# Attention in another order: transposes and values two steps behind the scores and between their rows, scans in 256-column parts from a queue, six probability rows

## The chip, the cores and the metric

The kernel runs on one core of a Trainium2 chip. The number to explain is the device time of one execution in microseconds (us). The engines are named as in the profile: PE multiplies matrices (PEld is its weight load, which overlaps it), DVE is the vector engine, ACT the scalar engine, POOL is GpSimd, SP issues DMAs. Before the change three runs took 2288.64 to 2288.95 us, median 2288.77 us.

## What is computed

One decoder layer over 1024 tokens of width 1024 in float32: a half-weight SwiGLU block, two attentions side by side with gates, another half-weight SwiGLU block, and a gated embedding. The change touches the attentions. Both have 8 heads of width 64, and queries are taken in blocks of 128 rows.

```python
# forgetting attention (fox), causal
logits = q @ k.T * scale + F[t] - F[s]          # F: running sum of log forget gates
out = softmax(logits) @ v
# stick-breaking attention (sb), strictly causal
z = q @ k.T * scale
after = reverse_cumsum(log_sigmoid(-z)) - log_sigmoid(-z)
out = exp(log_sigmoid(z) + after) @ v
```

The kernel does the second in products instead of logarithms: `T = sigmoid(z)`, `G = sigmoid(-z)`, and a running product of G from the right by a scan on DVE. Each float32 operand of a matmul is split in a high and a low part.

## The kernel before, in words

The layer runs as one program: first SwiGLU block, gates, projections, attention, merge of the branches, second SwiGLU block, embedding. In the SwiGLU, gate and output stages the code fixes the order on every engine; in attention a planner orders each engine's queue from the order of the code, except where `order("pe", ...)`, `order("dve", ...)` and `order("act", ...)` chain instructions by hand. The chain on DVE holds the scans and, in stick-breaking heads, the low parts of the transposed probabilities.

Attention goes through 16 heads, h = 0 to 15: 8 fox heads and then 8 sb heads. A head has four steps, c = 0 to 3. A step has two parts:

- `scores` (L1015 on) for two rows of 128 queries, i = 2c and 2c + 1, each with n = 128(i + 1) keys. PE multiplies q by the high and the low part of k (L1037, L1038). A fox row is then added to the forget sums and reduced on DVE (L1042), goes through exp on ACT (L1048), a reciprocal on DVE (L1049) and a multiplication on POOL (L1050). An sb row has two sigmoids on ACT (L1045 writes G, L1046 writes T), a mask on POOL (L1052), the scans on DVE (L1013) from G into a third tile R, and multiplications T by R on POOL (L1060, L1064).
- `apply` (L1074 on) for a step whose rows T are finished. From the last 256 keys to the first, PE transposes a block of 2 x 256 probabilities into a PSUM bank (L1089), ACT copies its high part into the tile PT (L1091) and DVE writes the low part (L1092, "the low" below). There are c + 1 such turns in a step. The values matmuls (L1111) of a block stand two turns later. At the end ACT and DVE take the sum out of the one bank `av` (L1133, L1134).

Before the change the apply of a step stands behind both score rows of the next step. The scans of a row are cut into two parts, `right` and `left`; those of the first row of a step are issued at once, and those of the second row go into a list `later`, one part behind each turn's low. So the DVE order in a turn is: low, scan part, next low. Two PSUM banks hold transposes (`pt`), three hold scores (`sc`), and four tiles T hold probability rows, which is two steps.

Between these, `fill()` puts matmuls of other units (projections L799 and L807, branch products L1360) into the PE order, a share of the head's fill at each call. A step calls it 7, 4, 5 and 6 times for c = 0 to 3. What is left at the end of a head is run out.

## Time and profile before

| what | us |
|---|---|
| median of three runs | 2288.77 |
| the profiled execution, its own time | 2287.47 |
| its span | 2285.6 |
| fox heads, 851 to 1123, length | 272 |
| sb heads but the last, 1123 to 1357.8, length | 234.8 |
| last sb head and the apply behind it, 1357.8 to 1407 | 49.2 |

The profiled execution is 1.3 us below the median, and the span begins and ends inside it. The stages outside 851 to 1407 us have their order fixed by hand; the granted clock of PE is 1.00 of full speed throughout. In the profile's rows a matmul counts as busy until its modelled end, while the next one starts earlier: a row of several matmuls tells the distance between them.

### The profile page before, as it was taken

The numbers are of one execution on the slowest core, as the hardware profiler recorded it, in microseconds if no ns is written. First come the engines' busy times: TensorE is split into PE (matmuls) and PEld (weight loads), VectorE is DVE, ScalarE is ACT, GpSimd is POOL, SyncE is SP. The second block draws the span as 40 slices with busy tenths as digits, with TensorE's granted clock in tenths as the row PEclk, the third lists the DMA queues.
The fourth block names the chain that finished last, engine by engine and source line by source line (L and its number), as shares of the span: only waits on it lengthen the run. The fifth ranks groups of instructions, "written<-read, shape, count | busy, mean of one in ns | idle before, by whom it ended". The sixth has DMA issues, their size and how long they took to land.

```text
span 2285.6 us, 30594 instructions
## 1 busy us (share of the span) xinstructions
PE 2242.3 (98%) x11402; PEld 1900.6 (83%) x11402; DVE 1498.9 (66%) x2264; ACT 999.5 (44%) x1787; POOL 805.7 (35%) x747
## 2 busy tenths in 40 slices
PE   8999999999999999999999989999999999999999
PEld 6888888888888899998788778888888888888887
DVE  8845454688877336566578786888745555778753
ACT  6333333333365445565656663246333333434431
POOL 2444444300011236566457554500535343200121
PEclk9999999999999999999999999999999999999999
DMA  3232323474233342233223346732423232656132
GB/s 139 102 116 93 115 93 115 174 277 170 84 128 130 120 144 72 64 103 88 70 47 83 93 125 203 263 133 74 138 79 129 79 129 79 252 196 220 62 104 83
DMA packets 184902, 283.87 MB, mean 124 GB/s; under 512 B 27945, under 2 KB 104105, under 8 KB 184754
## 3 DMA queue, kind: packets, MB, share of 16 engines
q1 hardware_dynamic: 184752, 281.92, 37.1%
q8 instruction: 90, 1.47, 0.3%
q14 instruction: 58, 0.48, 0.1%
q10 hardware_dynamic: 2, 0.00, 0.0%
HBM read 189.83 MB, written 75.27 MB: 116 GB/s over the span
## 4 chain that ended last, share of the span: by engine, by line
PE 87%; DVE 7%; ACT 3%; issue 1%; POOL 1%; DMA 1%; SPq 0%; DVEq 0%; ACTq 0%; POOLq 0%
PE ps L556 39%; PE ps L454 21%; PE ps L799 7%; PE ps L1555 4%; PE ps L1360 3%; PE ps L807 3%; DVE RN L1013 3%; PE ps L1111 2%; PE ps L506 2%; PE ps L1089 2%; DVE PT L1092 1%; PE ps L1037 1%; PE ps L1038 1%; PE ps L956 1%; PE ps L228 1%
## 5 line engine op out<-in xcount | busy, mean ns | idle before, releaser
L454 PE MATMUL ps<-H,H 128*128 128x512 f32 x2184 | 497.7, 389 | 1.2 <-DVE X L462 1.2
L454 PEld LDWEIGHTS ps<-H,H 128*128 128x128 f32 x2184 | 409.3, 188 | 86.7 <-issue 2.0
L556 PE MATMUL ps<-H,WL 128*128 128x512 f32 x1116 | 265.0, 389 | 0.8 <-ACT WL L105 0.8
L556 PEld LDWEIGHTS ps<-H,WL 128*128 128x128 f32 x1116 | 209.4, 188 | 44.7 <-ACT WL L105 1.2
L556 PE MATMUL ps<-H,Q 128*128 128x512 f32 x612 | 146.0, 389 | 0.0
L462 DVE SCALAR_TENSOR_TENSOR X<-ps,X 128x512 f32<-128x512 f32 x168 | 109.0, 685 | 50.9 <-PE ps L454 50.9
L556 PEld LDWEIGHTS ps<-H,Q 128*128 128x128 f32 x612 | 114.9, 188 | 23.9
L556 PE MATMUL ps<-X,WL 128*128 128x512 f32 x552 | 132.6, 389 | 0.0
L1092 DVE TENSOR_TENSOR PT<-ps,PT 128x512 fp32r<-128x512 f32 (+1 forms) x160 | 99.9, 630 | 49.6 <-ACT PT L1091 48.8
L139 POOL TENSOR_TENSOR WL<-RAW,WH 128x512 fp32r<-128x512 f32 (+1 forms) x84 | 98.1, 1191 | 67.8 <-ACT WH L129 44.5
L556 PEld LDWEIGHTS ps<-X,WL 128*128 128x128 f32 x552 | 103.6, 188 | 21.5
L1111 PE MATMUL ps<-PT,X 128*128 128x256 f32 (+1 forms) x640 | 103.0, 286 | 15.3 <-DVE PT L1092 11.9
L799 PE MATMUL ps<-WH,H 128*128 128x256 f32 x768 | 115.6, 287 | 0.6 <-ACT PT L962 0.3
L807 PE MATMUL ps<-H,WH 128*128 128x512 f32 x384 | 114.9, 408 | 0.0
L1091 ACT CAST PT<-ps 128x512 fp32r<-128x512 f32 (+1 forms) x160 | 87.1, 549 | 61.6 <-PE ps L1089 60.2
L219 POOL TENSOR_SCALAR ss<-ss 128x1 f32<-128x1 f32 x28 | 8.4, 298 | 297.2 <-ACT WL L215 231.9
L1111 PEld LDWEIGHTS ps<-PT,X 128*128 128x128 f32 x640 | 89.8, 190 | 27.6 <-DVE PT L1092 18.2
L556 PE MATMUL ps<-H,PT 128*128 128x512 f32 x456 | 108.8, 389 | 0.0
L1013 DVE TENSOR_TENSOR_SCAN RN<-GF,RN 128x127 f32<-128x127 f32 (+2 forms) x96 | 102.6, 1068 | 2.5
L799 PEld LDWEIGHTS ps<-WH,H 128*128 128x128 f32 x768 | 101.4, 190 | 2.1 <-ACT PT L962 0.5
L1089 PE MATMUL ps<-identf,T 128*128 128x128 f32 x576 | 90.6, 275 | 11.6 <-DVE PT L1092 9.9
L1050 POOL TENSOR_TENSOR T<-T,l 128x128 f32<-128x128 f32 (+3 forms) x64 | 73.1, 1148 | 78.6 <-DVE l L1049 77.2
(434 smaller groups left out, 4825.4 us busy)
## 6 DMA issues: line engine op xcount, KB each, us to landing
hidden<-PT SPq DMA_DIRECT2D x40, 512.0 KB, 3.1
WH<-in_ffn_w_gate_dram SPq DMA_DIRECT2D x38, 512.0 KB, 5.3
Q<-hidden SPq DMA_DIRECT2D x24, 512.0 KB, 7.1
hidden<-RN SPq DMA_DIRECT2D x22, 512.0 KB, 2.6
KH<-in_ffn_w_up_dram SPq DMA_DIRECT2D x20, 512.0 KB, 6.2
KL<-in_ffn_w_up_dram SPq DMA_DIRECT2D x20, 512.0 KB, 6.9
T<-in_ffn_w_down_dram SPq DMA_DIRECT2D x20, 512.0 KB, 4.2
X<-in_x_dram SPq DMA_DIRECT2D x16, 512.0 KB, 9.5
```

What stands on the lines that cost most here:

```text
L139: ins = eng_lo.tensor_sub(lo[part], raw[part], f(hi[part]))
L454: pe(nc.tensor.matmul(groups[g][t][:], act[:, a, k, t * P:(t + 1) * P], wt[:, b, k, :], start=(fresh and n == 0), stop=(i in (6, 1, 4) and ...
L462: nc.vector.scalar_tensor_tensor(xs, groups[g][t][:], scale, xs, ALU.mult, ALU.add)
L556: pe(nc.tensor.matmul(ps[:], hl[:, a, k, :], rhs(m, b, k), start=(first and i == 0), stop=(final and i == 11), skip_group_check=True))
L799: pe(nc.tensor.matmul(ps[:, :n], hT[t // 4](a, k)[:, (t % 4) * P:(t % 4 + 1) * P], w[k // 4][b][:, k % 4, :n], start=(i == 0), stop=(i == ...
L807: pe(nc.tensor.matmul(ps[:], w[a][:, k, :], hT[half](b, k), start=(i == 0), stop=(i == 23)))
L1013: order("dve", nc.vector.tensor_tensor_scan(*args))
L1089: pe(nc.tensor.transpose(ps[:, col:col + P], step["pr"][j][:, kb * P:(kb + 1) * P], identf[:]))
L1091: high = nc.scalar.copy(pt[:, 0, :width], ps[:, :width])
L1092: low = nc.vector.tensor_sub(pt[:, 1, :width], ps[:, :width], f(pt[:, 0, :width]))
L1111: pe(nc.tensor.matmul(o, lh, r, start=(kpair == c and i == 0), stop=(kpair == 0 and i == 3)))
L1555: pe(nc.tensor.matmul(ps, hT[t // 4](a, k)[:, (t % 4) * P:(t % 4 + 1) * P], pl["w"][d, k // 2][b][:, k % 2, cs], start=(i == 0), stop=(i = ...
```

## The change

Seven things are changed, nearly all inside attention.

1. `apply` runs two steps behind `scores`, not one, and its turns stand between the two score rows: 1, 2, 1, 1 turns for c = 0 to 3, the rest behind the second row. `scores` and `apply` become generators for this.
2. The scans are cut at multiples of 256 keys. The parts wait in a list `pend`, sorted by step and then from the right. `pop` issues one part, or two when more than five wait: once before each score row and once in each turn, ahead of the low. Before a row all parts of the step two back are popped, and in a turn all parts that its transposes or the two turns behind it need.
3. A scan writes into G itself; the tile R goes. G takes turns between the two pools that held G and R, so four rows of G are there instead of two. The segments of an sb row are scored from the right.
4. There are six tiles T instead of four and four tiles PT instead of five; two tiles of the gate stage move from PT to T, and the scratch area for software DMA shrinks from 4096 to 1024 bytes.
5. The last addition of an apply (L1134 before) is issued later, behind the next low or ahead of the next score row; in sb heads it joins the DVE chain.
6. The fill of a head is shared out anew, 0.27, 0.19, 0.27, 0.27 over 6, 7, 4, 5 calls.
7. The last head gets five branch units as fill instead of seven; the other five run beside the two applies that remain at the end.

The number of instructions on PE, ACT and SP stays. DVE gets 32 more scans (192 instead of 160), POOL 56 more multiplications (160 instead of 104).

First place, DVE in step c = 3 of sb head h = 11. SCALAR_TENSOR_TENSOR on L1013 is a scan, TENSOR_TENSOR PT a low, KL the low part of a key stack, Y the last addition. Before:

```order
L1013 SCALAR_TENSOR_TENSOR RN_11496<-GF_11495,mask_sb 128x128
L1013 SCALAR_TENSOR_TENSOR RN_11496<-GF_11495,RN_11496 128x383
L882 TENSOR_TENSOR KL_11274<-ps_11427,KH_11273 128x512
L1013 SCALAR_TENSOR_TENSOR RN_11496<-GF_11495,RN_11496 128x384
L1092 TENSOR_TENSOR PT_11556<-ps_11552,PT_11556 128x384
L1013 SCALAR_TENSOR_TENSOR RN_11535<-GF_11534,mask_sb 128x128
L1013 SCALAR_TENSOR_TENSOR RN_11535<-GF_11534,RN_11535 128x383
L1092 TENSOR_TENSOR PT_11572<-ps_11567,PT_11572 128x512
L1013 SCALAR_TENSOR_TENSOR RN_11535<-GF_11534,RN_11535 128x512
L1092 TENSOR_TENSOR PT_11586<-ps_11581,PT_11586 128x512
L1134 TENSOR_TENSOR Y_10845<-ps_11551,Y_10845 64x256
```

And now, in the same step:

```order
L1013 SCALAR_TENSOR_TENSOR RN_11446<-RN_11446 128x256
L1013 SCALAR_TENSOR_TENSOR GF_11412<-GF_11412 128x255
L1117 TENSOR_TENSOR PT_11514<-ps_11510,PT_11514 128x384
L1013 SCALAR_TENSOR_TENSOR RN_11446<-RN_11446 128x255
L1013 SCALAR_TENSOR_TENSOR GF_11493<-GF_11493,mask_sb 128x128
L1013 SCALAR_TENSOR_TENSOR RN_11528<-RN_11528,mask_sb 128x128
L1013 SCALAR_TENSOR_TENSOR RN_11528<-RN_11528 128x128
L1117 TENSOR_TENSOR PT_11549<-ps_11544,PT_11549 128x512
L1013 SCALAR_TENSOR_TENSOR GF_11493<-GF_11493 128x256
L1013 SCALAR_TENSOR_TENSOR RN_11528<-RN_11528 128x256
L1163 TENSOR_TENSOR Y_10800<-ps_11509,Y_10800 64x256
```

Three turns with their lows stood in this step and stand in the next head's first step now; of the rows' own scans (RN_11496, RN_11535 before, GF_11493, RN_11528 now) all stood here and 5 of 9 stand here now.

Second place, PE around the same step. L1037, L1050: q by the high part of k, L1038, L1051 by the low part; L1089, L1109: transposes; L807: fill. Before:

```order
L1037 MATMUL ps_11536<-KH_11083,Q_11082 128x512
L1038 MATMUL ps_11536<-KL_11084,Q_11082 128x512
L1037 MATMUL ps_11541<-KH_11083,Q_11082 128x512
L1038 MATMUL ps_11541<-KL_11084,Q_11082 128x512
L807 MATMUL ps_11522<-H_4504,WH_11267 128x512 x2
L807 MATMUL ps_11522<-H_4505,WH_11267 128x512 x2
L1089 MATMUL ps_11552<-identf,T_11402 128x128
L1089 MATMUL ps_11552<-identf,T_11432 128x128 x2
L807 MATMUL ps_11522<-H_4505,WH_11267 128x512 x2
L807 MATMUL ps_11522<-H_4504,WH_11267 128x512 x3
L1089 MATMUL ps_11567<-identf,T_11402 128x128
L1089 MATMUL ps_11567<-identf,T_11432 128x128
```

And now:

```order
L1109 MATMUL ps_11510<-identf,T_11312 128x128
L1109 MATMUL ps_11510<-identf,T_11356 128x128 x2
L807 MATMUL ps_11469<-H_4504,WH_11227 128x512 x3
L807 MATMUL ps_11469<-H_4505,WH_11227 128x512
L1050 MATMUL ps_11529<-KH_11024,Q_11023 128x512
L1051 MATMUL ps_11529<-KL_11025,Q_11023 128x512
L1050 MATMUL ps_11534<-KH_11024,Q_11023 128x512
L1051 MATMUL ps_11534<-KL_11025,Q_11023 128x512
L807 MATMUL ps_11469<-H_4505,WH_11227 128x512 x3
L807 MATMUL ps_11469<-H_4504,WH_11227 128x512
L1109 MATMUL ps_11544<-identf,T_11312 128x128
L1109 MATMUL ps_11544<-identf,T_11356 128x128
```

The scores of the step's second row now stand between two groups of transposes, which belong to the step two back.

The diff, cut to its core:

```diff
-BUFS = {"X": 2, "H": 4, "RAW": 2, "WH": 3, "WL": 3, "T": 4, "GF": 2, "RN": 2,
-        "Q": 2, "KH": 2, "KL": 2, "Y": 2, "PT": 5}
+BUFS = {"X": 2, "H": 4, "RAW": 2, "WH": 3, "WL": 3, "T": 6, "GF": 2, "RN": 2,
+        "Q": 2, "KH": 2, "KL": 2, "Y": 2, "PT": 4}
...
+    def pop(upto=None):
+        n = 1 + (len(pend) > 5)
+        while pend and (n if upto is None else pend[0][:2] <= upto):
+            pend.pop(0)[2]()
+            n -= 1
+    pend, late = [], []
+    def flush():
+        while late:
+            late.pop(0)()
...
-                G = slot("GF", [P, S])
-                R = slot("RN", [P, S])
-            for a in range(na):
+                G = slot(("GF", "RN")[i % 2], [P, S])
+            for a in range(na) if fox else range(na - 1, -1, -1):
...
-                if i % 2 and later is not None:
-                    later.extend(parts)
-                else:
-                    for part in parts:
-                        part()
+                def part(kp, T=T, G=G, n=n, d0=d0):
+                    c0 = kp * 256
+                    c1 = min(c0 + 256, n)
+                    z0 = max(c0, 1)
+                    if c1 == n:
...
+                    else:
+                        g = G[:, z0:c1][:, ::-1]
+                        scan(g, g, g, G[:, c1:c1 + 1], ALU.mult, ALU.bypass)
+                    nc.gpsimd.tensor_mul(T[:, c0:c1], T[:, c0:c1], G[:, c0 + 1:c1 + 1])
+                pend.extend((step["id"], -kp, lambda kp=kp, part=part: part(kp)) for kp in range(step["c"], -1, -1))
+                pend.sort(key=lambda e: e[:2])
...
+        for i in (2 * step["c"], 2 * step["c"] + 1):
+            pop((step["id"] - 2, 0))
+            pop()
+            flush()
+            row(i)
+            yield
...
         def turn_and_scan(kpair):
-            transposes(kpair)
-            if later:
-                later.pop(0)()
+            low = transposes(kpair)
+            pop()
+            pop((step["id"], 2 - kpair))
+            low()
+            flush()
             fill()
...
-            share = (7 / 22, 4 / 22, 5 / 22, 6 / 22) if fox else (0.14, 0.19, 0.29, 0.38)
+            share = (0.27, 0.19, 0.27, 0.27)
...
-                scores(step, take, later if prev is not None else None)
-                if prev is not None:
-                    apply(prev, take, later)
-                prev = step
+                rows = scores(step, take)
+                turns = apply(prev.pop(0), take) if len(prev) == 2 else iter(())
+                next(rows)
+                run(islice(turns, (1, 2, 1, 1)[c]))
+                run(rows)
+                run(turns)
+                prev.append(step)
...
-        apply(prev, lambda: run(islice(rest, 6)))
+        for step in prev:
+            run(apply(step, lambda: run(islice(rest, 6))))
+        flush()
```

More of the change, by code (lines that the diff above doesn't have):

```diff
@@ L1018, in scores, with row @@
         fox = step["fox"]
-        for i in (2 * step["c"], 2 * step["c"] + 1):
+        def row(i):
             n = (i + 1) * P
@@ L1123, in apply @@
                 values(kpair + 2)
-        for part in later:
-            part()
+            yield
         if c:
@@ L1133, in apply, with add @@
         nc.scalar.copy(ys, av[HD:P, :256])
-        nc.vector.tensor_add(ys, av[0:HD, :256], ys)
-        if hh == 1 and c == 3 and step["last"] is False:
-            nc.sync.dma_start(yd[Y["idx"]], Y["t"][:])
+        def add():
+            ins = nc.vector.tensor_add(ys, av[0:HD, :256], ys)
+            if not step["fox"]:
+                order("dve", ins)
+            if hh == 1 and c == 3 and step["last"] is False:
+                nc.sync.dma_start(yd[Y["idx"]], Y["t"][:])
+        late.append(add)
     FOX_PAIRS = [2, 3, 0, 1]
```

46 lines of the change are left out of this document (23 added, 23 removed).

## The prediction

> **What bounds the kernel now.** I read the page's busy shares and slices first, then the busy time by stretch, the waits of PE's weight load in attention, and one step instruction by instruction.
>
> ```profile
> PE 2242.3 (98%) x11402; PEld 1900.6 (83%) x11402; DVE 1498.9 (66%) x2264; ACT 999.5 (44%) x1787; POOL 805.7 (35%) x747
> ...
> PE   8999999999999999999999989999999999999999
> ...
> PEclk9999999999999999999999999999999999999999
> ```
>
> PE is the bound, at full clock, and its idle time is 2285.6 - 2242.3 = 43 us. Where it lies, by stretches (span and length, then busy us and count of PE, PEld, DVE, ACT, POOL): the gate stage, the fox heads, seven sb heads, the last sb head with its tail, and the merge.
>
> ```profile
> 720.00:851.00 131.00, 131.00 (x778) 116.14 (x777) 41.64 (x92) 53.72 (x96) 45.42 (x35) 1.00 0.42 136
> ...
> 851.00:1123.00 272.00, 260.19 (x1930) 244.77 (x1929) 158.84 (x535) 158.03 (x341) 159.24 (x162) 1.00 0.30 83
> 1123.00:1357.80 234.80, 221.23 (x1330) 190.67 (x1330) 187.33 (x263) 143.33 (x309) 143.01 (x169) 1.00 0.32 84
> 1357.80:1407.00 49.20, 45.15 (x252) 37.64 (x251) 40.92 (x56) 25.02 (x52) 28.91 (x32) 1.00 0.65 206
> ...
> 1407.00:1500.00 93.00, 93.00 (x412) 77.01 (x411) 66.88 (x82) 22.61 (x30) 34.81 (x30) 1.00 0.68 239
> ```
>
> Beside attention PE has no gap; inside it 11.8 + 13.6 + 4.1 = 29.5 us. A busy PE hides part of each stall, since a matmul counts until its modelled end. The weight load, which stands ahead of the array, shows the stalls whole. Its waits from 851 to 1123, then from 1123 to 1407 (us, times, longest):
>
> ```profile
> PEld ps L1089 <- DVE PT L1092: 4.9, 4, 1.5
> PEld ps L1111 <- DVE PT L1092: 4.9, 9, 1.4
> PEld ps L1111 <- ACT PT L1091: 4.0, 5, 2.0
> PEld ps L1089 <- POOL T L1050: 1.6, 1, 1.6
> ...
> PEld ps L1111 <- DVE PT L1092: 13.3, 16, 1.3
> PEld ps L1089 <- DVE PT L1092: 11.1, 15, 2.1
> ```
>
> So 15.4 us in the fox heads and 24.4 us in the sb heads: together 40 us, and nearly all of it is PE waiting for a low. That is the most a new order can give. Where in a head: the four steps of sb head h = 11.
>
> ```profile
> 1226.60:1233.60 7.00, 6.94 (x49) 6.03 (x48) 4.70 (x9) 3.60 (x9) 4.87 (x7) 1.00 0.58 143
> 1233.60:1238.20 4.60, 4.60 (x27) 3.90 (x26) 2.95 (x6) 2.99 (x7) 1.56 (x3) 1.00 0.07 15
> 1238.20:1246.00 7.80, 7.80 (x45) 6.81 (x45) 7.07 (x12) 5.79 (x13) 5.68 (x7) 1.00 0.29 67
> 1246.00:1259.60 13.60, 11.34 (x61) 9.06 (x60) 11.87 (x12) 6.82 (x14) 9.56 (x9) 1.00 0.35 78
> ```
>
> PE idles only in c = 3, where DVE is busy 11.87 of 13.60 us; in c = 1 it is busy 2.95 of 4.60. DVE has time, in the wrong steps. Its instructions in that step, then PE's and POOL's around them (start, length):
>
> ```profile
> 1248.18 1.20 DVE L1013 TENSOR_TENSOR_SCAN RN<-GF,mask_sb 128x128 f32<-128x128 f32 x1 [1.08 <-ACT GF L1045]
> 1249.42 1.86 DVE L1013 TENSOR_TENSOR_SCAN RN<-GF,RN 128x383 f32<-128x383 f32 x1
> 1251.20 0.66 DVE L882 TENSOR_TENSOR KL<-ps,KH 128x512 fp32r<-128x512 f32 x1
> 1251.79 1.77 DVE L1013 TENSOR_TENSOR_SCAN RN<-GF,RN 128x384 f32<-128x384 f32 x1
> 1253.48 0.53 DVE L1092 TENSOR_TENSOR PT<-ps,PT 128x384 fp32r<-128x384 f32 x1
> ...
> 1254.95 1.02 DVE L1013 TENSOR_TENSOR_SCAN RN<-GF,RN 128x383 f32<-128x383 f32 x1
> ...
> 1256.47 2.01 DVE L1013 TENSOR_TENSOR_SCAN RN<-GF,RN 128x512 f32<-128x512 f32 x1
> 1258.40 0.66 DVE L1092 TENSOR_TENSOR PT<-ps,PT 128x512 fp32r<-128x512 f32 x1
> ```
>
> ```profile
> 1249.79 0.49 PE L1089 MATMUL ps<-identf,T 128*128 128x128 f32 x3
> ...
> 1251.27 0.60 PE L1089 MATMUL ps<-identf,T 128*128 128x128 f32 x4
> ...
> 1254.06 0.66 PE L1089 MATMUL ps<-identf,T 128*128 128x128 f32 x4 [1.26 <-DVE PT L1092]
> ...
> 1254.79 1.09 PE L807 MATMUL ps<-H,WL 128*128 128x512 f32 x4
> ```
>
> ```profile
> 1247.81 2.66 POOL L139 TENSOR_TENSOR WL<-RAW,WH 128x512 fp32r<-128x512 f32 x2
> ...
> 1256.12 1.28 POOL L1060 TENSOR_TENSOR T<-T,RN 128x511 f32<-128x511 f32 x1 [1.11 <-DVE RN L1013]
> ```
>
> The transposes of 1249.79 end at 1250.28, but their low starts at 1253.48, behind 1.86 + 0.66 + 1.77 us of DVE work. There are two `pt` banks, so the third group waits for that low. And the scans are stretched: 383 columns take 1.02 us undisturbed and 1.86 us beside POOL's weight split; the 512-column scan begins 0.35 us into a POOL multiplication that ends at 1257.40, and ends 1.08 us after it.
>
> **The change part by part.** *Cost of the cutting.* Undisturbed prices in the same heads:
>
> ```profile
> 1238.25 0.75 DVE L1013 TENSOR_TENSOR_SCAN RN<-GF,RN 128x256 f32<-128x256 f32 x1
> 1240.11 0.43 DVE L1013 TENSOR_TENSOR_SCAN RN<-GF,mask_sb 128x128 f32<-128x128 f32 x1
> ...
> 1239.50 0.74 POOL L1064 TENSOR_TENSOR T<-T,RN 128x256 f32<-128x256 f32 x1
> ```
>
> From 256 to 383 columns a scan grows by 0.27 us, 2.1 ns a column, so 0.21 us is fixed. The scanned columns stay the same, so 32 more scans add 32 x 0.21 = 6.8 us to DVE, 0.85 us a head. On POOL 256 to 511 columns are 0.74 to 1.28 us, 0.20 us fixed: 56 x 0.20 = 11 us, 1.4 us a head; POOL is busy 143 of 235 us and nobody but late lows waited for it. If that cover is gone, the transposes wait for T (none of the quoted sb waits is of that kind).
>
> *Moving scans and turns, sb heads.* I count the DVE rows of the new order at 0.43 (mask, 128), 0.75 (255, 256), 0.53 to 0.66 (low), 0.4 (Y) and 0.66 (KL): 5.8, 7.4, 3.6 and 6.7 us for c = 0 to 3, in all 23.5. The old order counted alike has 8.2 us in c = 3 and 22.7 in the head; recorded are 26.59, so about 3.9 us a head are scans held up beside POOL, nearly all of it in c = 3. PE's need in the new steps: 72 fill matmuls a head at (1.09 - 0.39)/3 = 0.23 us from start to start, shared 0.27, 0.19, 0.27, 0.27; scores of 0.35, 0.8, 1.2 and 1.7 us; a transpose at 0.11 and a value matmul at 0.12 us. That is 7.4, 7.5, 6.4 and 7.9 us. With one held-up microsecond in each step DVE needs 6.8, 8.4, 4.6 and 7.7. The worst step is now c = 1, 0.9 us over PE. It was c = 3, 11.87 us against 10.6 that PE needed there (0.38 x 72 x 0.23 + 1.7 + 2.6 for the turns of c = 2). Expected stall in a head: 0.9 us in c = 1 and 0.2 in each other step, where the last low still ends shortly ahead of its values: 1.5 us, 12 in eight heads, where 24.4 are now. So 12 us go. Bounds: all 24.4 go, or none.
>
> *The low behind the scans.* Now each low stands behind one or two parts (0.75 to 1.5 us), put in the time in which PE transposes and ACT copies. Behind a late low wait the transposes two turns on and the values; behind the values the copy of `av`. This is counted above; if DVE is late as a whole it is the slow rival.
>
> *Fox heads.* There are no scans and `pop` does nothing. What changes is that T is ready a step earlier, and that ACT has one exp between two highs where it had two:
>
> ```profile
> 1104.43 0.71 ACT L1048 ACTIVATE T<-T,m 128x512 f32<-128x512 f32 x1
> 1105.05 0.19 ACT L1048 ACTIVATION_READ_ACCUMULATOR T<-T,m 128x1 f32 x1
> 1105.14 0.46 ACT L1091 CAST PT<-ps 128x384 fp32r<-128x384 f32 x1
> ...
> 1105.65 1.09 PE L1111 MATMUL ps<-PT,X 128*128 128x256 f32 x4 [1.54 <-ACT PT L1091]
> ```
>
> The POOL wait (1.6) and the ACT waits (4.0) should mostly go; the 9.8 us behind DVE's lows stay, as their order there is not changed and a turn of c = 1 has less fill than the old c = 0 (0.19/7 against 7/22/7 of a head's). I take 5 of 15.4 us; bounds +3 (less cover) and -12.
>
> *Edges.* The tail has two applies, with five branch units beside them instead of three; PE's work is the same, and DVE is busy 40.9 of 49.2 us there, so I take 0, between -3 and +3. The sb rows' G must now be free of POOL's multiplication of two steps back, not of the scan; the pop ahead of the row and a step of distance cover it. Slots T and PT of the other stages: PE has 131 of 131 us in the gate stage, and a split runs four products of 12 x 0.23 us ahead of its use, which hides a wait for a slot: 0, at most +3. The later store of a Y pair sits in SP's queue less than a step longer; loads behind it have no PE waiter in the lists above: 0. The software DMA scratch is used by no queue that the page lists as moving data: 0.
>
> *Sum.* -12 - 5 + 0 = -17 us, against the profiled 2287.47 us 2270.5. The median of the runs is 1.3 us above the profiled run, so **2271.8 us**.
>
> **A rule weighed.** A scan and a multiplication that overlap delay each other: the held-up 512 columns ended 1.08 us after POOL's end, where alone they take 0.75 + 256 x 2.1 ns = 1.29. So 0.2 us, the fixed part, had run beside POOL, and cutting adds only such parts. [...]
>
> **The rivals.**
> - *Nearly all waits go.* PE's need of the four new steps is 29.2 us where the head now lasts 33.0. Of the 40 us some 33 go: 2288.8 - 33 = 2256. Against it: DVE needs 27.5 of those 29.2 us.
> - *The waits only move.* DVE stays at its limit in c = 1 and c = 0, the added 6.8 us eat the better balance, and fox gives 5: 2284. For it: c = 1 has 0.45 us of fill a turn and four lows.
> - *Slower: scans and multiplications queue for each other.* If their sum is what limits the sb heads, the added 6.8 + 11 us come on top, and lows behind two parts pass it to PE: 2288.8 + 18 - 5 = 2302. It decides where the held-up time passes 1.4 us in c = 1: then 7.4 + 1.4 is 1.3 us over PE's 7.5, as far as c = 3 is over now. For it: DVE and POOL together are busy 21.4 us in 13.6 of c = 3. Against it: in c = 1 they fill 4.5 of 2 x 4.6 us, and lows, which read PSUM, keep 0.66 us beside POOL.
>
> **How the numbers follow.** Chances: forecast 0.50 (its own range 2263 to 2281), nearly all 0.12, only moved 0.20, slower 0.18. A run tells a change from none at about 0.2%, 4.6 us, below 2284.2 and above 2293.4. Faster: 0.50 + 0.12 + half of 0.20 = 0.72; same: 0.07 of the moved and 0.03 of the slow case, 0.10; slower 0.18. The range 2254 to 2297 leaves out part of the first rival and the upper part of the last.
>
> **What would show it.** Right: in the sb heads the waits of PEld behind the low fall to about 12 us, none of the steps has DVE above 90% with PE idle over 1 us, no scan is over 1.6 us, DVE's busy sum over attention grows by less than 7 us; in the fox heads waits behind ACT and POOL vanish. Wrong: a 256-column scan takes 1.2 us on the mean, the transposes wait for POOL's multiplications, or ACT waits for a free G; then the slow rival has it. Waits for a PT slot outside attention would make the zero of that edge wrong.

## The result, and the profile after

The changed kernel took 2274.68 us (median of four runs, 2273.32 to 2275.51), beside 2288.7 us for the kernel before in the same comparison: a ratio of 0.9939, 95% interval 0.9921 to 0.9956. The forecast was 2271.8 us. The execution that was profiled took 2275.51 us, 12.0 us less than the profiled one of before.

The page's busy shares and granted clock of the changed kernel (each digit is a slice of 57 us, in tenths):

```profile
PE 2241.4 (99%) x11402; PEld 1905.0 (84%) x11402; DVE 1490.0 (66%) x2296; ACT 1000.1 (44%) x1787; POOL 806.5 (35%) x803
...
PEclk9999999999999999999999999999999999999999
```

The span is 2273.8 us, so PE idles for 32 us where it idled for 43. PE's busy sum is the same to 1 us. The clock's digits hide spells of a lower clock, which a finer cut shows below. Then the same stretches as before the change, fox heads, seven sb heads, last sb head with its tail (span and length, busy us and count of PE, PEld, DVE, ACT, POOL, then the granted clock):

```profile
851.00:1119.50 268.50, 258.86 (x1910) 244.34 (x1908) 159.15 (x532) 156.76 (x337) 158.54 (x160) 0.99 0.31 84
1119.50:1339.00 219.50, 216.22 (x1325) 190.03 (x1324) 170.02 (x285) 140.86 (x307) 140.55 (x211) 1.00 0.33 85
1339.00:1395.00 56.00, 49.88 (x275) 42.60 (x275) 46.67 (x70) 27.76 (x58) 34.55 (x47) 0.94 0.66 218
```

The seven sb heads give the gain, 234.8 to 219.5 us, the fox heads a little, 272 to 268.5, and the last head gives half of the gain back, 49.2 to 56.0. To read this rightly one has to look at the counts: the fox heads hold 20 matmul records fewer than before (1910 against 1930), the last stretch 23 more (275 against 252). With `apply` two steps behind, the three turns of one more step with c = 2 wait at the end of each stretch. That is the 2.6 us that the prediction gave for those turns. It leaves the fox heads, and enters and leaves the seven sb heads alike.

From the first score matmul of each head in both traces, and with that shift taken out:

| | before | after | difference | the 2.6 us put back | forecast |
|---|---|---|---|---|---|
| fox heads | 271.6 | 268.2 | -3.4 | -0.8 | -5 |
| sb heads 8 to 14 | 234.2 | 219.7 | -14.5 | -14.5 | -12 (all sb heads) |
| last sb head and tail | 49.3 | 56.1 | +6.8 | +4.2 | 0 (edges) |

With 0.6 us by which attention begins earlier this makes -11.7 us; attention ends at 1395.3 where it ended at 1407.1. Behind it both kernels take the same 878.5 us.

What PE's weight load waits for in the seven sb heads (us in total, times, longest), before the change (1123 to 1357.8 us) and then after it (1119.5 to 1339 us):

```profile
PEld ps L1111 <- DVE PT L1092: 11.7, 14, 1.2
PEld ps L1089 <- DVE PT L1092: 8.6, 12, 1.8
```

```profile
PEld ps L1135 <- DVE PT L1117: 5.8, 11, 1.1
```

It waited 20.3 us behind the low before, in 26 places; now 5.8 in 11. All waits of the transposes for a `pt` bank (L1089 before, L1109 now) are gone. The same sb head as before, h = 11, in its four steps:

```profile
1215.70:1223.50 7.80, 7.80 (x49) 6.66 (x48) 7.39 (x11) 3.46 (x9) 7.80 (x10) 1.00 0.49 123
1223.50:1231.80 8.30, 8.13 (x52) 6.83 (x51) 7.05 (x13) 4.80 (x10) 4.64 (x9) 1.00 0.29 64
1231.80:1238.30 6.50, 6.50 (x37) 5.63 (x36) 3.94 (x7) 5.43 (x12) 2.72 (x6) 1.00 0.07 15
1238.30:1246.10 7.80, 7.80 (x44) 6.64 (x44) 7.18 (x11) 5.44 (x12) 6.54 (x9) 1.00 0.74 134
```

The step c = 3 lasted 13.60 us with 11.87 us of DVE; it now lasts 7.80 with 7.18, and PE has no gap in it. The load of DVE now follows the work that PE has in each step.

The gain isn't even over the heads. The first sb head gave 4.7 of the 14.5 us (34.6 to 29.9): no scans come into it from the fox heads, and only 19 of its 24 scans run before it ends, so DVE is busy 20.9 us in it instead of 27.3. The other six heads gave 1.6 us each. At the other end the last head has 30 scans to run where it had 20.

In the fox heads, among others:

```profile
PEld ps L1135 <- ACT PT L1111: 5.0, 6, 1.4
PEld ps L1135 <- DVE PT L1117: 4.4, 9, 0.7
```

And in the last sb head, where nothing of the kind stood before:

```profile
PEld ps L1109 <- POOL T L1065: 4.0, 1, 4.0
PEld ps L1109 <- POOL WL L139: 2.4, 1, 2.4
```

The place, instruction by instruction (start, length):

```profile
1345.16 0.63 PE L1109 MATMUL ps<-identf,T 128*128 128x128 f32 x4 [2.01 <-POOL WL L139]
...
1348.99 4.43 DVE L106 TENSOR_TENSOR H<-X,H 128x1024 fp32r<-128x1024 f32 x3
...
1355.02 0.53 DVE L1117 TENSOR_TENSOR PT<-ps,PT 128x384 fp32r<-128x384 f32 x1
...
1355.69 1.09 PE L1109 MATMUL ps<-identf,T 128*128 128x128 f32 x4 [3.58 <-DVE PT L1117]
```

Three splits of Y into high and low part (L106) stand on DVE in step c = 1 of the last head, 4.43 us in one piece. Behind them wait scans and the low of 1355.02, and behind these the transposes. (The list above puts this wait down to POOL's mask, L1065, but that ended at 1354.67 us; the low, which frees the `pt` bank, ended at 1355.55.) PE stands for 3.58 us. The transposes that follow take 1.09 us for four where four take 0.60 elsewhere, and the clock granted around them is lower:

```profile
1350.00:1360.00 10.00, 6.42 (x30) 5.46 (x29) 9.96 (x16) 4.34 (x9) 6.82 (x10) 0.71 0.38 128
1360.00:1370.00 10.00, 10.00 (x56) 8.87 (x56) 6.43 (x12) 5.70 (x15) 3.37 (x8) 0.95 0.40 134
```

Ten us at 0.71 and ten at 0.95 are 2.9 + 0.5 = 3.4 us of PE's full speed lost. A part of that lies in the gap itself, where PE had nothing to do; the rest comes on top of it.

### The profile page after: what moved, and what is told of

It reads as the page before. It is cut to its first block, busy times and chain, and to the rows that moved or that the text cites. A ratio compares the mean times of both kernels' runs of the same rounds, so it can differ in the third digit from the quotient of the medians.

```text
span 2273.8 us, 30750 instructions
## 1 busy us (share of the span) xinstructions
PE 2241.4 (99%) x11402; PEld 1905.0 (84%) x11402; DVE 1490.0 (66%) x2296; ACT 1000.1 (44%) x1787; POOL 806.5 (35%) x803
## 4 chain that ended last, share of the span: by engine, by line
PE 91%; DVE 5%; ACT 2%; issue 1%; DMA 0%; POOL 0%; SPq 0%; ACTq 0%; DVEq 0%
PE ps L556 39%; PE ps L454 21%; PE ps L799 8%; PE ps L807 4%; PE ps L1591 4%; PE ps L1396 3%; PE ps L1135 3%; PE ps L1109 2%; PE ps L506 2%; PE ps L1051 1%; PE ps L1050 1%; PE ps L956 1%; PE ps L228 1%; DVE PT L1117 1%; DVE RN L1013 1%
## 5 line engine op out<-in xcount | busy, mean ns | idle before, releaser
L807 PE MATMUL ps<-H,WH 128*128 128x512 f32 x384 | 114.3, 408 | 0.6 <-ACT PT L926 0.6
L1135 PEld LDWEIGHTS ps<-PT,X 128*128 128x128 f32 x640 | 91.8, 193 | 22.3 <-DVE PT L1117 11.3
L556 PEld LDWEIGHTS ps<-H,PT 128*128 128x128 f32 x456 | 85.5, 188 | 17.8
L355 POOL TENSOR_TENSOR PT<-GF,RN 128x512 f32<-128x512 f32 x20 | 33.6, 1680 | 184.7 <-DVE GF L710 184.7
L1063 POOL TENSOR_TENSOR T<-T,l 128x128 f32<-128x128 f32 (+3 forms) x64 | 73.5, 1150 | 72.1 <-DVE l L1062 70.2
```

What stands on the lines that cost most here:

```text
L556: pe(nc.tensor.matmul(ps[:], hl[:, a, k, :], rhs(m, b, k), start=(first and i == 0), stop=(final and i == 11), skip_group_check=True))
L807: pe(nc.tensor.matmul(ps[:], w[a][:, k, :], hT[half](b, k), start=(i == 0), stop=(i == 23)))
L1063: nc.gpsimd.tensor_mul(T[:, :n], T[:, :n], l[:].broadcast_to([P, n]))
L1135: pe(nc.tensor.matmul(o, lh, r, start=(kpair == c and i == 0), stop=(kpair == 0 and i == 3)))
```

## The experiments

Each kernel is the changed one with the edit shown (e6 and e12 have that of e1 as well). This table gives the time, the ratio to the kernel before that ran beside it, and the lengths as above, each from its own trace. The last column is the time that this one execution loses to the clock through attention, at most: the sum of (1 - granted clock) x 2 us over windows of 2 us. Such losses come in portions of some 1.7 us and partly by chance (see the last section), so a difference in this column has to be weighed when two kernels are compared.

| kernel | us | ratio, 95% interval | fox | sb 8 to 14 | last and tail | clock |
|---|---|---|---|---|---|---|
| changed | 2274.68 | 0.9939 [0.9921, 0.9956] | 268.2 | 219.7 | 56.1 | 5.1 |
| e1_splits | 2269.93 | 0.9922 [0.9907, 0.9937] | 266.6 | 219.6 | 51.8 | 0.0 |
| e2_one_behind | 2299.87 | 1.0054 [1.0039, 1.0069] | 286.6 | 230.8 | 45.2 | 6.8 |
| e3_no_queue | 2301.21 | 1.0058 [1.0043, 1.0073] | 268.2 | 244.9 | 56.7 | 15.3 |
| e4_low_first | 2280.69 | 0.9970 [0.9959, 0.9981] | 266.5 | 225.2 | 56.1 | 5.1 |
| e11_pop_one | 2281.90 | 0.9973 [0.9964, 0.9983] | 266.6 | 225.5 | 56.9 | 3.4 |
| e10_add_now | 2285.89 | 0.9993 [0.9984, 1.0002] | 268.2 | 227.4 | 60.1 | 10.3 |
| e7_no_mul | 2268.57 | 0.9913 [0.9898, 0.9928] | 268.1 | 215.9 | 53.3 | 1.7 |
| e8_parts512 | 2276.55 | 0.9950 [0.9935, 0.9964] | 266.6 | 223.3 | 54.7 | 0.0 |
| e5_old_share | 2287.74 | 0.9997 [0.9988, 1.0007] | 275.1 | 226.8 | 54.1 | 8.5 |
| e6_shares | 2266.45 | 0.9902 [0.9885, 0.9918] | 267.4 | 217.5 | 50.5 | 5.1 |
| e12_sb_share | 2267.94 | 0.9915 [0.9900, 0.9930] | 268.2 | 218.0 | 51.3 | 1.7 |
| e9_no_table | 2268.31 | 0.9918 [0.9901, 0.9934] | 261.1 | 219.4 | 56.3 | 3.4 |

The trace of the kernel before loses nothing to the clock in attention. Beside e9 to e12 that kernel took 2287.31 us, about 1 us less than beside the others; their ratios account for it. In e2_one_behind the 2.6 us of turns stand where they stood before the change, and 5.4 us of branch products, which stand in "last and tail" elsewhere, run behind its tail.

**The last head: e1_splits.** The three Y splits go from step c = 1 of the last head to c = 2 and c = 3.

```diff
-    Y_AT = {(14, 0): ((), range(4)), (14, 3): ((0, 1), (4, 5)), (15, 0): ((2, 3), (6,)), (15, 1): ((4, 5, 6), ())}
+    Y_AT = {(14, 0): ((), range(4)), (14, 3): ((0, 1), (4, 5)), (15, 0): ((2, 3), (6,)), (15, 2): ((4, 5), ()), (15, 3): ((6,), ())}
```

> The changed kernel, but the last three splits of Y tiles stand two in c = 2 and one in c = 3 of the last head, not all three in its c = 1. If the 4.43 us of splits on DVE inside the step with four turns are what holds the lows up there (PE idle 3.58 us at one place, then a granted clock of 0.71 for 10 us), some 5 us go: about 2270 us, and the clock is 1.00 between 1340 and 1370 us. If the last head is limited by DVE's whole load (49.8 of 52.8 us busy), the splits cost the same anywhere: 2274 to 2275 us.

The last head and tail fell from 56.1 to 51.8 us. With the 2.6 us of the extra turns taken off that is 49.2, the length before the change. The same two stretches of the last head, in this kernel:

```profile
1348.00:1358.00 10.00, 9.34 (x58) 7.84 (x57) 9.96 (x17) 8.58 (x18) 8.31 (x12) 1.00 0.14 47
1358.00:1368.00 10.00, 9.94 (x53) 8.29 (x51) 9.87 (x16) 7.87 (x17) 7.59 (x11) 1.00 0.49 165
```

PE idles 0.7 us in the first of them instead of 3.6, and the clock stays at 1.00. The splits in that step were the whole loss of the last head, gap and clock together. The fox heads are shorter by 1.6 us because a spell of lower clock, which the changed kernel's trace has there, is absent.

**The distance of two steps: e2_one_behind.** The turns stay between the rows, but those of the step directly behind; calls and shares as they were before the change.

```diff
-            share = (0.27, 0.19, 0.27, 0.27)
+            share = (7 / 22, 4 / 22, 5 / 22, 6 / 22) if fox else (0.14, 0.19, 0.29, 0.38)
...
-                state[0] += total * share[state[2]] / (6, 7, 4, 5)[state[2]]
+                state[0] += total * share[state[2]] / (7, 4, 5, 6)[state[2]]
...
-                turns = apply(prev.pop(0), take) if len(prev) == 2 else iter(())
+                turns = apply(prev.pop(0), take) if len(prev) == 1 else iter(())
                 next(rows)
-                run(islice(turns, (1, 2, 1, 1)[c]))
+                run(islice(turns, (2, 1, 1, 1)[c]))
```

> The changed kernel with apply one step behind the scores instead of two, and with the old shares of the fill; queue, parts and the place of the turns between the rows stay (2, 1, 1, 1 turns behind the first row). If the even load on DVE is what counts, the step c = 0, which then has the four turns and the scans of c = 3 together (some 7.5 us of DVE against 6.2 of PE), stalls again by 1 to 2 us a head: about 2283 us. If the distance only gives POOL and ACT time, which nobody waited for long, 2276 us.

Both expectations were far off. PE's waits through the whole of attention:

```profile
PEld ps L1109 <- POOL T L1063: 19.2, 12, 3.7
PEld ps L1109 <- POOL T L1082: 16.3, 18, 2.1
PEld ps L1135 <- DVE PT L1117: 6.8, 17, 0.6
```

Lows hold the values up for only 6.8 us; the transposes wait for POOL's multiplication of T, 19.2 us in the fox heads (L1063) and 16.3 in the sb heads (L1082); PE's own list gives 16.1 and 9.1. A turn that stands between two rows comes too early for the rows of one step back. The 25 us above the changed kernel aren't all due to the distance, since the shares differ too. The old shares alone, in e5_old_share below, give 2287.74 us; beside that kernel the distance costs 12.1 us (2299.87 - 2287.74), 9 of them in the fox heads (with the 2.6 us of turns taken off) and 4 in the sb heads. So it isn't a refinement of the new order: without it, at the old shares, the kernel is slower than before the change.

**The queue: e3_no_queue, e4_low_first, e11_pop_one.** First, all parts of a row are issued as soon as its scores are.

```diff
             step["pr"].append(T)
+            pop((step["id"], 0))
             fill()
```

> The changed kernel, but all scan parts of a row are issued right behind its scores; nothing waits in the queue. By the sums over a step little changes: DVE gets 7.5 us and about 1 of hold-ups in c = 3 against 7.9 of PE, and less in the others: about 2277 us. If the order inside the step counts, the lows of c = 2 and c = 3 stand behind a block of 2.5 to 3 us of scans, PE waits about 1 us in two steps of each of eight heads, and the time is about 2288 us.

It cost twice what was expected, 26.5 us, all in the sb heads, which became longer than before the change (244.9 against 234.2). PE's main wait through attention (line numbers are one higher in this kernel):

```profile
PEld ps L1136 <- DVE PT L1118: 32.7, 25, 3.7
```

All parts of a row, four in c = 3, stand ahead of a low, and PE waits up to 3.7 us for it. In the changed kernel this wait is 11.3 us in all, and the longest 1.1. The trace loses 15.3 us to the clock, the changed one 5.1, so some 10 of the 26.5 us are clock behind these waits. Cutting the scans is of no use without spreading them.

Second, the low goes ahead of the parts that are taken in its turn, as before the change.

```diff
             low = transposes(kpair)
+            low()
             pop()
             pop((step["id"], 2 - kpair))
-            low()
             flush()
```

> The changed kernel with the low of a turn ahead of the scan parts, not behind them. If the load of a step decides, 2275 to 2278 us. If the scan is needed to fill the time in which PE transposes and ACT copies (0.35 + 0.6 us and two hand-overs, about 1.1 us), DVE idles some 0.5 us in each of 80 turns and lacks 5 us a head, against 1.7 us of slack: 2290 us or more, and DVE's idle time behind ACT's high parts is above 60 us.

The answer lay between the two: 6.0 us slower, with 5.5 us more in the sb heads (1.7 of these are a spell of lower clock, which the changed kernel has in its fox heads instead). The lows' groups of DVE over the sb heads (busy us and mean ns, then idle time ahead and what ended it) in the changed kernel and in this one:

```profile
L1117 DVE TENSOR_TENSOR PT<-ps,PT 128x512 fp32r<-128x512 f32 (+1 forms) x89 | 55.3, 623 | 20.9 <-ACT PT L1111 20.5
```

```profile
L1117 DVE TENSOR_TENSOR PT<-ps,PT 128x512 fp32r<-128x512 f32 (+1 forms) x89 | 55.6, 625 | 42.2 <-ACT PT L1111 41.9
```

With the low first, DVE stands 21 us longer waiting for ACT's high, time in which it could scan; ahead of the last addition it stands 10 us less (15.2 instead of 25.6). So a late low is less harmful than an idle DVE, and the prediction's placing of parts "in the time in which PE transposes and ACT copies" is confirmed with a size of 6 us.

Third, never two parts at a time.

```diff
-        n = 1 + (len(pend) > 5)
+        n = 1
```

> The changed kernel, taking always one part from the queue at a place and never two. If the rate of one part for each place is enough, the time stays within 1 us of 2274.7 us. If parts gather and are then forced out in a bunch where a row needs them, a four-turn step pays about 0.3 us in each of 8 heads, and the total is 2277 to 2279 us.

The sb heads grew by 5.8 us, more than twice the 2.4 us expected for bunching. PE's own waits in the sb heads 8 to 14, and ACT's row for G in step c = 3 of head 11:

```profile
PE ps L1135 <- DVE PT L1117: 3.8, 5, 1.6
PE ps L1109 <- DVE PT L1117: 3.0, 6, 0.9
```

```profile
1225.15 0.49 ACT L1058 ACTIVATE GF<-ps 128x384 f32<-128x384 f32 x1 [1.89 <-POOL T L1082]
```

PE waits 6.8 us for lows, 2.4 in the changed kernel. The parts that are left run late, and so do POOL's multiplications behind them, which read G; ACT waits for a free G, 5.8 us in five places of these heads where the changed kernel has 1.2 in two. Its high copy stands behind that sigmoid (1225.91 us), the low behind the high and the scans (1226.55), and the transposes that need the low's bank start at 1227.23. The queue has to run ahead of its deadlines, not just to meet them.

**The held-back addition: e10_add_now.**

```diff
         late.append(add)
+        flush()
```

> The changed kernel, with the last addition of a head done at once and not held back. If holding it back does nothing for the time, as my sum had it, within 1 us of 2274.7 us. If the addition in front of the scans delays the first probabilities of the next head, each of 16 heads loses about 0.4 us and the total is 2279 to 2281 us.

11 us slower, level with the kernel before. The prediction had left this part of the change without a price. DVE in the same step of head 11, in this kernel and then in the changed one:

```profile
1226.45 0.42 DVE L1163 TENSOR_TENSOR Y<-ps,Y 64x256 f32<-64x256 f32 x1 [1.12 <-ACT Y L1160]
1226.80 0.83 DVE L1013 TENSOR_TENSOR_SCAN GF<-GF,mask_sb 128x127 f32<-128x127 f32 x1
```

```profile
1222.93 0.47 DVE L1013 TENSOR_TENSOR_SCAN GF<-GF,mask_sb 128x127 f32<-128x127 f32 x1
1224.12 0.42 DVE L1163 TENSOR_TENSOR Y<-ps,Y 64x256 f32<-64x256 f32 x1 [0.72 <-ACT Y L1160]
```

The addition must wait for the values, whose last low has just been written, and for ACT's copy. Done at once it stops DVE for 1.1 us with a scan ready behind it; held back, that scan runs first, and DVE stands for 0.7. The sb heads 8 to 14 lose 7.7 us, unevenly, from nothing to 3.4 us a head, and the clock falls in the last head (0.87 over its 60 us). Of the 11 us 5 are clock: the trace loses 10.3 us, that of the changed kernel 5.1.

**Cutting and POOL: e7_no_mul, e8_parts512.** First, POOL's multiplications of T by the running product are left out. The stick-breaking outputs then lack that factor; everything else runs.

```diff
                         scan(g, g, g, G[:, c1:c1 + 1], ALU.mult, ALU.bypass)
-                    nc.gpsimd.tensor_mul(T[:, c0:c1], T[:, c0:c1], G[:, c0 + 1:c1 + 1])
```

> The changed kernel without POOL's multiplications of T by G in the sb heads; that part of the result is left out. If scans that are held up beside POOL make up what DVE lacks in c = 1, the mean of a 256-column scan falls from 0.87 to about 0.75 us, DVE's busy time in the sb heads falls by 15 to 20 us, and 5 to 8 us of PE's stall go: 2267 to 2270 us. If DVE's order and its own durations set the stall, 2273 to 2275 us.

6.1 us faster than the changed kernel, which is the expected time, but 3.4 of it are clock (1.7 us lost against 5.1). The sb heads 8 to 14 gave 3.8 us, less than the 5 to 8 expected. The scans tell more. Their groups before the change:

```profile
L1013 DVE TENSOR_TENSOR_SCAN RN<-GF,RN 128x127 f32<-128x127 f32 (+2 forms) x96 | 102.6, 1068 | 2.5
...
L1013 DVE TENSOR_TENSOR_SCAN RN<-GF,mask_sb 128x128 f32<-128x128 f32 (+1 forms) x64 | 40.3, 630 | 9.5 <-ACT GF L1045 8.9 <-POOL WL L139 0.3
```

In the changed kernel:

```profile
L1013 DVE TENSOR_TENSOR_SCAN RN<-RN 128x256 f32<-128x256 f32 (+3 forms) x80 | 60.6, 757 | 1.3
...
L1013 DVE TENSOR_TENSOR_SCAN GF<-GF 128x255 f32<-128x255 f32 (+1 forms) x48 | 39.8, 828 | 0.2
L1013 DVE TENSOR_TENSOR_SCAN RN<-RN,mask_sb 128x128 f32<-128x128 f32 x32 | 18.8, 588 | 2.1 <-ACT RN L1058 1.8
L1013 DVE TENSOR_TENSOR_SCAN GF<-GF,mask_sb 128x128 f32<-128x128 f32 (+1 forms) x32 | 16.6, 518 | 1.7 <-ACT GF L1058 1.2
```

And without the multiplications:

```profile
L1013 DVE TENSOR_TENSOR_SCAN RN<-RN 128x256 f32<-128x256 f32 (+3 forms) x80 | 52.8, 660 | 1.3
L1013 DVE TENSOR_TENSOR_SCAN GF<-GF 128x255 f32<-128x255 f32 (+1 forms) x48 | 36.8, 768 | 0.2
L1013 DVE TENSOR_TENSOR_SCAN GF<-GF,mask_sb 128x128 f32<-128x128 f32 (+1 forms) x32 | 16.1, 504 | 1.7 <-ACT GF L1058 1.2
...
L1013 DVE TENSOR_TENSOR_SCAN RN<-RN,mask_sb 128x128 f32<-128x128 f32 x32 | 13.9, 434 | 2.0 <-ACT RN L1058 1.8
```

The eight sb heads scan 8 x 4608 = 36864 columns. By the prediction's prices (2.1 ns a column, 0.21 us for each scan) 192 scans would take 77.4 + 40.3 = 117.7 us undisturbed, 160 scans 111.0. Recorded are 119.6 us without the multiplications, 135.8 with them, and 142.9 before the change. So the price is right to 2 us. The rest is time in which scans are held up beside POOL: in the changed kernel's trace a 256-column scan takes 0.74 us with nothing on POOL, and 0.94 on the mean and 1.70 at most with POOL busy beside it. In the changed kernel it is 18 us, of which 16 go with the multiplications; before the change it was 32 us, with fewer scans and fewer multiplications. How much of the 32 us lies beside POOL's other work, such as its weight split, no run shows.

Second, parts of 512 columns, in the same queue.

```diff
-                    c0 = kp * 256
-                    c1 = min(c0 + 256, n)
+                    c0 = kp * 512
+                    c1 = min(c0 + 512, n)
...
-                pend.extend((step["id"], -kp, lambda kp=kp, part=part: part(kp)) for kp in range(step["c"], -1, -1))
+                pend.extend((step["id"], -min(2 * kp + 1, step["c"]), lambda kp=kp, part=part: part(kp)) for kp in range(step["c"] // 2, -1, -1))
```

> The changed kernel with the scans cut at multiples of 512 keys instead of 256: 144 scans instead of 192 and 96 multiplications instead of 160. If the fixed cost of a part is what the cutting brings (0.21 us on DVE, 1.3 us a head less), about 2272 us. If fine parts are needed so that a low never waits behind much, scans of 1.3 us and more in one turn bring stalls back: 2279 to 2284 us.

1.9 us above the changed kernel, and the intervals of the ratios overlap, so the time alone doesn't tell them apart. The sb heads 8 to 14 are 3.6 us longer. But this trace loses nothing to the clock, and that of the changed kernel 5.1 us: at the same clock the coarser parts cost some 6 us between the two profiled executions. What the weight load waits for from the sb heads to the end of attention:

```profile
PEld ps L1135 <- DVE PT L1117: 12.5, 13, 2.3
PEld ps L1109 <- DVE PT L1117: 3.3, 1, 3.3
```

That is 15.8 us behind lows, where the changed kernel has 6.9. The 144 scans take 136.4 us together, 28.8 more than 77.4 + 30.2: the coarser cut saves 10.1 us of fixed parts and pays 10.7 us of held-up time. So cutting is free on DVE, and what it gives is that a low waits for less scan at a time.

**The shares of the fill: e5_old_share, e6_shares, e12_sb_share.** First the shares from before the change.

```diff
-            share = (0.27, 0.19, 0.27, 0.27)
+            share = (7 / 22, 4 / 22, 5 / 22, 6 / 22) if fox else (0.14, 0.19, 0.29, 0.38)
```

> The changed kernel with the old shares of the fill (7/22, 4/22, 5/22, 6/22 in fox heads, 0.14, 0.19, 0.29, 0.38 in sb heads). If the fill has to follow the load that DVE has in a step, c = 0 of the sb heads has 7.4 - 0.13 x 16.6 = 5.2 us of PE work against 6.8 of DVE and stalls by about 1.5 us a head, c = 1 as now: 2274.7 + 11 = 2286 us, and the fox heads lose or gain less than 3. If moving the scans alone did it: 2275 us.

The whole gain went, as expected. The main waits through attention:

```profile
PEld ps L1135 <- DVE PT L1117: 14.1, 27, 1.3
PEld ps L1109 <- DVE PT L1117: 6.7, 3, 5.4
```

PE's work no longer follows DVE's, and the lows are late again. The sb heads 8 to 14 take 226.8 us, 7.4 less than before the change and 7.1 more than after: taken in this order, the rest of the change and the shares each give half there. The old order with the new shares wasn't run. The fox heads take 275.1; most of the 6.9 us more lie in the second head, with its one wait of 5.4 us. The clock takes 5.1 us in them (0.75, 0.91, 0.94 and 0.89 in the four stretches of 10 us from 890), where it takes 1.7 in the changed kernel.

Second, other shares and the splits of e1.

```diff
-            share = (0.27, 0.19, 0.27, 0.27)
+            share = (0.23, 0.31, 0.2, 0.26) if fox else (0.26, 0.25, 0.22, 0.27)
...
-    Y_AT = {(14, 0): ((), range(4)), (14, 3): ((0, 1), (4, 5)), (15, 0): ((2, 3), (6,)), (15, 1): ((4, 5, 6), ())}
+    Y_AT = {(14, 0): ((), range(4)), (14, 3): ((0, 1), (4, 5)), (15, 0): ((2, 3), (6,)), (15, 2): ((4, 5), ()), (15, 3): ((6,), ())}
```

> The kernel with the later Y splits (2269.9 us), and more of the fill for c = 1, the step with four turns: 0.31 of a fox head and 0.25 of an sb head, taken from the other steps. If PE stalls in c = 1 because a turn has only 0.45 us of fill there (fox heads: the last turns wait for the high and the low part, about 10 us in all; sb heads: DVE needs 8.4 us against 7.5), 3 to 6 us go: 2264 to 2267 us. If the waits follow from ACT's table loads and DVE's sum, they only move to other steps: 2269 to 2272 us.

2266.45 us, the fastest kernel of the study, 8.2 us below the changed one. The time was as expected. Beside e1 the sb heads gave 2.1 us and the last head 1.3. The fox heads seem to give nothing (267.4 against 266.6), but here they lose 3.4 us to the clock and in e1 none, so at the same clock they are some 2.6 us shorter. Their waits fell too, behind ACT's highs from 5.0 to 3.7 us and behind lows from 4.4 to 3.2.

Third, the old fox shares with still more of the sb fill in c = 1, and the same splits.

```diff
+            share = (0.27, 0.19, 0.27, 0.27) if fox else (0.25, 0.29, 0.19, 0.27)
```

> The kernel with the Y splits moved and the filling shared anew (2266.5 us), with the fox shares of the changed kernel put back and more of the sb filling in c=1: shares 0.25, 0.29, 0.19, 0.27. If a step stalls only where VectorE's work in it is longer than TensorE's, TensorE's c=1 becomes about 8.5 us against 8.4 of VectorE, c=2 about 4.9 against 4.4, and the sb heads 8 to 14 fall below 217 us: 2264 to 2266 us in all. If c=2 or c=0 begins to stall instead, 2268 to 2270 us.

2267.94 us lies between the two expectations, and the sb heads, at 218.0 us, didn't fall below 217. They take 1.6 us less than in e1 and 0.5 more than in e6, so between these two shares they hardly differ. Which step stalls in its place wasn't settled.

**The fox heads: e9_no_table.** The sigmoid of two blocks of gate rows becomes an exponential, so the kernel leaves out the true values of those gates; the count of operations is the same, but ACT loads no table there, where it has eight loads of 1.28 us in the changed kernel.

```diff
-            order("act", nc.scalar.activation(g[:], ps[:], AF.Sigmoid))
+            order("act", nc.scalar.activation(g[:], ps[:], AF.Exp if m < 14 else AF.Sigmoid))
```

> The changed kernel, with the sigmoid of two blocks of gate rows, those computed inside the fox heads, replaced by an exponential (the gates of those blocks are wrong, their amount of work is the same). The exponential's table stays loaded, so four pairs of table loads of 1.28 us each leave ScalarE in the fox heads. If what is left of TensorE's waits in the fox heads (5.0 us behind ScalarE, 4.4 us behind VectorE between 848 and 1119.5) starts at these loads, the fox heads shorten from 268.2 to 264 to 265 us and the total is about 2271 us. If the waits come from VectorE's own load, the fox heads stay within 1 us of 268.2 and the total at 2274 to 2275 us.

The fox heads shortened by 7.1 us, more than the 3 to 4 expected; heads 3, 4 and 7 by 0.7, 2.1 and 4.1. ACT of the changed kernel in head 7, and PE behind it:

```profile
1096.12 1.28 ACT L926 ACT_TABLE_LOAD   x1
...
1097.41 0.60 ACT L926 ACTIVATE PT<-ps 128x512 f32<-128x512 f32 x1
...
1098.03 1.28 ACT L1061 ACT_TABLE_LOAD   x1
...
1100.05 1.05 ACT L1111 CAST PT<-ps 128x512 fp32r<-128x512 f32 x2
...
1100.66 0.39 PE L1135 MATMUL ps<-PT,X 128*128 128x256 f32 x1 [1.17 <-ACT PT L1111]
```

A sigmoid between two exponentials takes ACT 2.56 us of loads (2 x 1.28, the next ACTIVATE follows each within 0.02 us), and two highs stand behind it. PE waits 1.17 us. About 1.7 us of the 7.1 are clock: the stretch from 1100 to 1110 us ran at 0.83 in the changed kernel and at 1.00 in this one. The remaining 5.4 us belong to the four pairs of loads; against traces of the same fox heads without such a spell (266.6 us, as in e1) the difference is 5.5.

## Why the prediction was right, and where it was not

- *What bounds the kernel, and the sb heads.* Right. The waits behind the low fell from 24.4 to 6.9 us in the eight heads, where a fall to about 12 was forecast, and seven heads gave 14.5 us where eight were to give 12. In head 11 DVE was forecast at 6.8, 8.4, 4.6 and 7.7 us for the four steps and took 7.4, 7.1, 3.9 and 7.2; the worst step went from c = 3 to c = 1, the longest one at 8.3 us and the only one with a PE gap (0.2 us), as said. But PE has 8.1 us of work in it where 7.5 were counted, so it is long by PE's own work more than by DVE's. The term of 12 us was too small for two reasons, whose shares no run gives: held-up time was taken as unchanged at about a microsecond a step, while it fell from 32 to 18 us over all heads; and all heads were taken alike, while the first gave 4.7 us and the other six 1.6 each, close to the 1.5 forecast.
- *That the order does it.* The prediction ascribed the 12 us to the balance of DVE's load and priced the parts of the order inside one sum. The runs give each part a size: without the two-step distance +12 us (at the old shares), without the queue +26.5 (10 of it clock), the low ahead of the parts +6.0, one part at a time about +7, the addition at once about +11 (5 of it clock), the old shares +13 (3 of it clock). They add up to far more than the gain, so they aren't independent: each one, taken away, makes DVE or POOL late by itself. The held-back addition had no price in the prediction at all. That the transposes may wait for POOL, and ACT for a free G, stands in it as a sign of being wrong, without a price; e2 and e11 show both.
- *Cutting.* The price of the cutting is right (without POOL's multiplications 192 scans take 119.6 us, by the price 117.7). The step that held them to be a net cost was wrong by sign: the scans together fell by 7.1 us, and e8 shows why, since longer parts in the same queue are held up 10.7 us more. Scans over 1.6 us still occur, but only just: the longest are 1.70.
- *The fox heads.* The term -5 was mis-sized: -0.8 us with the turns put back. 1.7 us of lost clock lie in that; the traces without this spell (266.6 us) give -2.4, half of the term. The reason failed too. The prediction said that the waits behind ACT and POOL would go and those behind the low stay. POOL's did go; those behind the low fell from 9.8 to 4.4 us, and those behind ACT's highs grew from 4.0 to 5.0. That one exp stands between two highs where there were two doesn't help where two table loads stand there, which e9 shows. Of the 40 us of waits that the prediction called nearly all lows, 5.6 stood behind ACT and POOL here.
- *Edges.* The tail's term 0 was wrong: +4.2 us, outside its bounds of 3. "PE's work is the same, and DVE is busy 40.9 of 49.2 us there" took DVE's load over the whole stretch, the very thing that the prediction avoids elsewhere; its splits of Y now fall into a four-turn step together with four lows and the scans between them. e1 shows that this was all of it. The other zeros (slots T and PT, SP's queue, the scratch) held: the stages ahead of attention take 0.6 us less than before, those behind it the same.
- *The rivals.* The waits didn't merely move in the sb heads, and not all of them went. The slower rival fell: scans are held up beside multiplications (e7: 16 us of held-up time go with the multiplications), but this didn't add the new instructions to the path: 88 more of them came with 14 us less of held-up time (18 us instead of 32). That the multiplications are delayed too, as the prediction had it, isn't seen in the changed kernel's trace: one of 256 columns takes 0.79 us on the mean beside a scan and 0.78 without one.

Between the profiled executions the change is -12.0 us, where -17 was forecast: the sb heads were better by 2.5, fox heads and last head worse by 4.2 each, and 0.6 came from ahead of attention. The medians differ by 2.1 us more, -14.1, since the profiled run of before lay 1.3 us below its median and that of after 0.8 above; so the forecast missed by only 2.9 us. That it came so close is in part luck: terms that missed by 2.5 to 4.2 us went both ways, and the two profiled executions lie 2.1 us closer together than the medians.

## What to carry to other kernels

When an engine whose order is fixed serves another one, compare their loads step by step and not over the whole: the gain here came from giving PE work in the steps in which DVE has some, and from a queue that keeps DVE from waiting with work at hand. When work moves to another step, list what else already stands there on every engine, above all at the last round of a loop, where the filling differs. A wait cost more than its length here: with the one of 3.58 us in the changed kernel's last head up to 3.4 us went to the clock. Before two kernels that lie a few microseconds apart are compared, take off what each trace lost to the clock.

## What the runs showed of the hardware that was not expected

In these traces PE's granted clock fell to about a half for some 3.4 us (1.7 us lost), or twice that, at short gaps. In the fox heads of e12_sb_share, where PE waited twice, 1.18 and 0.34 us, up to 910.92 us (windows of 2 us, columns as above):

```profile
911.00:913.00 2.00, 2.00 (x12) 2.00 (x13) 1.24 (x4) 0.56 (x2) 0.84 (x1) 0.59 0.46 110
913.00:915.00 2.00, 2.00 (x12) 2.00 (x12) 1.47 (x5) 1.25 (x4) 0.40 (x1) 0.55 0.33 74
915.00:917.00 2.00, 2.00 (x20) 2.00 (x19) 0.74 (x5) 0.97 (x3) 0.00 (x0) 1.00 0.88 202
```

PE is busy throughout, with 12 matmuls in 2 us where it has 20 at full clock. The head is 35.4 us long instead of 33.8. Eight kernels here run the same fox heads (the changed one, e1, e3, e4, e7, e8, e11 and e12) and have this pair of waits at two places. Four of the 16 places are followed by such a spell: in e3, e7 and e12 at the first place, in the changed kernel at the second; e1_splits, with the very same waits (1.18 and 0.34), has none. The fox heads take 268.1 or 268.2 us in the four traces with a spell and 266.5 or 266.6 in the four without. So a gap of that size was followed by the drop at some places and not at others, and 1.6 us here or there between two kernels means little. The gap of 3.58 us in the changed kernel's last head goes with a longer spell, at most 3.4 us lost; it begins before PE starts again (the window from 1354 to 1356 us stands at 0.56). The spell at the changed kernel's second place is at 0.50 in the window from 1102 to 1104 us, behind 1.5 us of waiting in two pieces (1.17 and 0.34). The kernel before the change has no such spell in attention, with waits of PE's weight load of up to 2.1 us; why, stays open.
